# A hybrid decoder block on one core: zero products at the start, a new order of the first loads, and a split last tile

## The chip, the cores and the metric

The kernel runs on one core of a Trainium2 chip. The metric is the device time of one execution in microseconds. Five engines work beside each other, each through its own instructions in order: TensorE (PE: products; PEld: loading of stationary tiles), VectorE (DVE), ScalarE (ACT), GpSimd (POOL) and SyncE (SP, which here only issues transfers). Engines wait for each other and for transfers by semaphores.

## What is computed

One layer of a decoder on 256 tokens with 16 meta tokens ahead of them, width 2048, all in float32:

```
xn = rmsnorm(h, norm1)
u = xn @ w_in                       # 11776 columns: attention q, k, v; retention q, k, v; gates
a = sliding_window_attention(...) @ w_attn_br
r = retention(...) @ w_ret_br
h = h + (sigmoid(gate_a) * a + sigmoid(gate_r) * r) @ w_out
g, up = split(rmsnorm(h, norm2) @ w_gate_up)
h = h + (silu(g) * up) @ w_down
out = rmsnorm(h, norm_f)[:, 128:]   # the meta tokens are dropped
```

## The kernel before

All weights (some 280 MB) are streamed once. Every float32 operand is kept as a high and a low half, and a product of two operands is three products of halves: high by high, high by low, low by high. A `Group` is 512 columns of one weight matrix over its whole contraction. `load` brings chunks of four 128-row contraction tiles by 512 columns (1 MB, three buffers `raw`), `split` makes the halves: ScalarE casts `hi` (L116), VectorE subtracts to get `lo` (L117). `multiply` does half a chunk, a *unit*. For most groups (kind "w") the weights are stationary and 256 or 272 tokens move, and a unit is four contraction tiles by 256 columns; for `w_out` and `w_down` (kind "x") the tokens are stationary and 512 columns move, and a unit is two contraction tiles by 512 columns.

The loop at the end of the kernel goes over all units in order; `ahead` loads and splits some units before they are multiplied. A scheduler then orders each engine's instructions; each engine keeps that order on the chip and waits where a semaphore says so.

The first group (attention keys and values, columns from 1536 of `w_in`) needs the tokens transposed, scaled by `norm1` and split. `norm_chunk(q)` does that for four contraction tiles: per tile one transpose of the 16 meta rows `mt` (L224) and two of the 256 rows of `xt` (L226), into an `aux` buffer (two of these), then ScalarE writes the high half of `xn` (L211) and VectorE the low half (L212). `gains` transposes the norm's weights (L206). The loads of `x` and meta rows come in column ranges between those of the weights, all from SP (L95 to L102, L194 to L200); small tables and the decay table of the retention (`dec`, 1.1 MB, L432) are issued by POOL. `squares` and `norm_end` compute the reciprocal roots `r1`, which the first group's evacuation (`evac_akv`) multiplies in.

At the end, the last group's two token tiles are multiplied one after the other (`toks`), so that the first is finished while the second is multiplied. `evac_down` adds the residual (L630), ScalarE sums squares (L632), `finish` scales and stores (L650 to L662).

## Time and profile before

| | |
|---|---|
| median of 3 runs | 1606.47 us (1604.6 to 1606.73) |
| profiled execution: span from first to last instruction | 1603.7 us |
| profiled execution: own time beside the span | not listed apart |
| PE busy | 1585.0 us, 99% |
| PEld busy | 1390.9 us, 87% |
| DVE busy | 908.6 us, 57% |
| ACT busy | 728.8 us, 45% |
| transfers | 290.64 MB, mean 181 GB/s |

The busy time of PE says that the engine had a product under way, not that it ran at its peak. The span is 2.8 us below the median of the runs. An engine other than PE can matter only where PE waits for it, and such places are found in the list of waits and in the order in time.

### The profile page before, as it was taken

How to read it: one execution, taken by the hardware profiler on the slowest of the kernel's cores; microseconds unless marked ns; L12 is line 12 of the kernel's file. 1: busy time of each engine (PE TensorE's matmuls, PEld its weight loads, DVE VectorE, ACT ScalarE, POOL GpSimd, SP SyncE). 2: the span in 40 equal slices, each digit the busy share in tenths (PEclk: the TensorE clock that was granted, in tenths of full speed). 3: DMA queues.
4: the chain of work that ended last, by engine and by line, in shares of the span. 5: the costliest groups of instructions: out<-in, count | busy, mean ns of one | idle time of the engine just before them, and what ended most of it. 6: DMA issues, size and time to landing. Idle time of an engine off the chain costs nothing.

```text
span 1603.7 us, 22417 instructions
## 1 busy us (share of the span) xinstructions
PE 1585.0 (99%) x9268; PEld 1390.9 (87%) x9268; DVE 908.6 (57%) x1089; ACT 728.8 (45%) x928; POOL 53.4 (3%) x79
## 2 busy tenths in 40 slices
PE   7999999999999999999999999999999999999997
PEld 6999989999988888888888888888888888888886
DVE  4656655465546656565655566656666566454453
ACT  6444444344444444444444444444454444344343
POOL 0212000100000000000000000000000000000000
PEclk9999999999999999999999999999999999999999
DMA  8645444355445555557555555565555656555553
GB/s 276 201 155 168 141 132 132 131 186 182 134 146 194 184 184 185 192 193 245 184 183 175 193 184 185 184 203 190 184 187 185 205 186 210 185 190 194 192 184 105
DMA packets 191702, 290.64 MB, mean 181 GB/s; under 512 B 6289, under 2 KB 98033, under 8 KB 191345
## 3 DMA queue, kind: packets, MB, share of 16 engines
q1 hardware_dynamic: 188480, 280.12, 52.5%
q0 software_dynamic: 1392, 5.94, 1.2%
q10 hardware_dynamic: 1728, 3.16, 0.6%
q8 instruction: 72, 1.18, 0.3%
q14 instruction: 30, 0.24, 0.0%
HBM read 287.08 MB, written 2.12 MB: 180 GB/s over the span
## 4 chain that ended last, share of the span: by engine, by line
PE 96%; DMA 1%; issue 1%; DVE 1%; ACT 0%; SPq 0%; POOL 0%; POOLq 0%; DVEq 0%; ACTq 0%
PE ps L139 34%; PE ps L140 18%; PE ps L159 7%; PE ps L157 7%; PE ps L158 7%; PE ps L145 5%; PE ps L144 5%; PE ps L143 5%; PE ps L137 2%; DMA raw<-in_w_in_dram 1%; PE ps L136 1%; PE aux L407 1%; PE aux L355 1%; PE aux L501 1%; PE aux L385 0%
## 5 line engine op out<-in xcount | busy, mean ns | idle before, releaser
L117 DVE TENSOR_TENSOR lo<-raw,hi 128x1024 fp32r<-128x1024 f32 (+1 forms) x530 | 651.2, 1230 | 541.2 <-ACT hi L116 532.7
L116 ACT CAST hi<-raw 128x1024 fp32r<-128x1024 f32 (+1 forms) x530 | 554.5, 1047 | 683.5 <-PE ps L139 321.8
L139 PE MATMUL ps<-hn,hi 128*128 128x512 f32 x1320 | 460.3, 391 | 0.0
L140 PE MATMUL ps<-hn,lo 128*128 128x256 f32 x1320 | 372.1, 282 | 0.0
L139 PEld LDWEIGHTS ps<-hn,hi 128*128 128x128 f32 x1320 | 247.8, 188 | 51.0
L139 PE MATMUL ps<-xn,hi 128*128 128x512 f32 x720 | 255.1, 396 | 0.0
L140 PEld LDWEIGHTS ps<-hn,lo 128*128 128x128 f32 x1320 | 249.5, 189 | 1.9
L143 PE MATMUL ps<-xn,hi 128*128 128x272 f32 (+1 forms) x704 | 203.1, 291 | 1.5 <-ACT hi L116 1.5
L140 PE MATMUL ps<-xn,lo 128*128 128x256 f32 x720 | 204.2, 284 | 0.0
L144 PE MATMUL ps<-xn,hi 128*128 128x272 f32 (+1 forms) x704 | 203.5, 290 | 0.0
L145 PE MATMUL ps<-xn,lo 128*128 128x272 f32 (+1 forms) x704 | 203.1, 289 | 0.0
L139 PEld LDWEIGHTS ps<-xn,hi 128*128 128x128 f32 x720 | 135.5, 188 | 29.7 <-issue 0.2
L159 PE MATMUL ps<-hi,ff 128*128 128x512 f32 x352 | 139.3, 396 | 0.0
L158 PE MATMUL ps<-lo,ff 128*128 128x512 f32 x352 | 139.3, 396 | 0.0
L157 PE MATMUL ps<-hi,ff 128*128 128x512 f32 x352 | 139.3, 396 | 0.0
L140 PEld LDWEIGHTS ps<-xn,lo 128*128 128x128 f32 x720 | 135.8, 189 | 2.3 <-issue 1.3
L143 PEld LDWEIGHTS ps<-xn,hi 128*128 128x128 f32 x704 | 132.9, 190 | 3.8 <-ACT hi L116 1.9
L144 PEld LDWEIGHTS ps<-xn,hi 128*128 128x128 f32 x704 | 133.5, 190 | 3.0 <-issue 2.8
L145 PEld LDWEIGHTS ps<-xn,lo 128*128 128x128 f32 x704 | 133.4, 190 | 1.9 <-issue 1.8
L541 DVE TENSOR_TENSOR t<-ps,t 128x512 f32<-128x512 f32 x84 | 58.2, 692 | 68.1 <-ACT t L540 68.0
L540 ACT COPY t<-ps 128x512 f32<-128x512 f32 x84 | 49.3, 587 | 86.5 <-PE ps L137 84.0
L139 PE MATMUL ps<-r_hl,hi 128*128 128x512 f32 x240 | 84.1, 394 | 0.0
(198 smaller groups left out, 1496.0 us busy)
## 6 DMA issues: line engine op xcount, KB each, us to landing
raw<-in_w_in_dram SPq DMA_DIRECT2D x91, 1024.0 KB, 5.0
raw<-in_w_gate_up_dram SPq DMA_DIRECT2D x176, 512.0 KB, 4.4
raw<-in_w_down_dram SPq DMA_DIRECT2D x44, 1024.0 KB, 5.0
raw<-in_w_ret_br_dram SPq DMA_DIRECT2D x16, 1024.0 KB, 5.1
raw<-in_w_out_dram SPq DMA_DIRECT2D x16, 1024.0 KB, 5.0
raw<-in_w_attn_br_dram SPq DMA_DIRECT2D x8, 1024.0 KB, 5.0
bias<-tbd POOLq DMA_DIRECT2D x4, 544.0 KB, 8.9
h<-in_x_dram ACTq DMA_DIRECT2D x4, 512.0 KB, 6.1
```

What stands on the lines that cost most here:

```text
L116: g.last_split = nc.scalar.copy(out=hi[:, j], in_=src[:, j])
L117: nc.vector.tensor_tensor(out=lo[:, j], in0=src[:, j], in1=hi[:, j].bitcast(F32), op=ALU.subtract)
L139: mm(out=full, lhsT=wh, rhs=xhl, start=first, stop=False)
L140: mm(out=ps[:, ct, 0:S], lhsT=wl, rhs=xhi, start=False, stop=False)
L143: mm(out=o, lhsT=wh, rhs=xhi, start=first, stop=False)
L144: mm(out=o, lhsT=wh, rhs=xlo, start=False, stop=False)
L145: mm(out=o, lhsT=wl, rhs=xhi, start=False, stop=last)
L157: mm(out=o, lhsT=xlo[:, tok], rhs=hi[:, k, :], start=kt == 0, stop=False)
L158: mm(out=o, lhsT=xhi[:, tok], rhs=lo[:, k, :], start=False, stop=False)
L159: mm(out=o, lhsT=xhi[:, tok], rhs=hi[:, k, :], start=False, stop=kt == nk - 1)
L540: nc.scalar.copy(out=t, in_=ps[:, :, S:2 * S])
L541: nc.vector.tensor_tensor(out=t, in0=ps[:, :, 0:S], in1=t, op=ALU.add)
```

## The change

- *Zero products.* `warm` multiplies a tile of zeros (`idle`, bfloat16, set by VectorE) into a spare accumulator `blank`, nine times ahead of the first transposes and twice behind the first x transposes, in the order of the code.
- *First loads.* In the first group's first chunk the four weight tiles come one by one, with 256 columns of x ahead of the first and the third; later chunks come in halves of two tiles. The meta rows come in two loads from ACT's queue, with 128 partitions each. The decay table is loaded by SP behind the first chunk of group 3, no longer by POOL at the start. `norm2` is loaded later.
- *First units.* For the first group (`pairs`) a unit is two contraction tiles by 512 columns; both accumulators are filled together, and evacuated after the last unit.
- *Meta rows.* Two transposes bring all meta rows (`norm_meta`); one multiply, one cast and one subtraction make their halves for all sixteen contraction tiles. `norm_pair` transposes x alone, two contraction tiles into one `aux` buffer. The meta tokens' norm is summed through a product with a `pick` matrix.
- *Last columns.* The second token tile of the last group is multiplied in two halves of 256 columns (`LAST`), each evacuated by `evac_last`; only the last half stands behind the last product.

In the changed kernel the cast of weights is at L129, the subtraction at L130, the first group's products at L146 to L148, the high half of `xn` at L236 and the low half at L237.

```diff
+    idle = const.tile([128, 512], BF16, name="idle")
+    nc.vector.memset(idle, 0.0)
...
     def load(g, c):
...
+        if g is groups[0]:
+            if c == 0:
+                for k in range(4):
+                    if k % 2 == 0:
+                        load_x(128 * k, 128 * k + 256)
+                    nc.sync.dma_start(out=raw[:, k, :], in_=rows[:, k, c0:c0 + 512])
+            else:
+                load_x(512 * c, 512 * (c + 1))
+                for k in (0, 2):
+                    nc.sync.dma_start(out=raw[:, k:k + 2, :], in_=rows[:, k:k + 2, c0:c0 + 512])
...
+        if g is groups[3] and c == 0:
+            with tc.issue_after(last.ins):
+                nc.sync.dma_start(out=r_state["dec"], in_=c_dec)
...
-    def multiply(g, c, half, toks=(0, 1)):
+    def multiply(g, c, half, toks=(0, 1), a=0, b=512):
...
+        if g.pairs:
+            if c == 0 and half == 0:
+                g.ps = [psm.tile([128, 2, 512], F32, name="ps") for _ in range(2)]
+            for k in range(2):
+                kt = 4 * c + 2 * half + k
...
+                for ct in range(4):
...
+                    mm(out=o, lhsT=wh, rhs=xhi, start=first, stop=False)
+                    mm(out=o, lhsT=wh, rhs=xlo, start=False, stop=False)
+                    m = mm(out=o, lhsT=wl, rhs=xhi, start=False, stop=last)
...
+    blank = psm.tile([128, 2, 512], F32, name="ps")
+    def warm(n):
+        for _ in range(n):
+            mm(out=blank[:, 0, :], lhsT=idle[:, 0:128], rhs=idle, start=True, stop=True)
+    def norm_meta():
+        gains(0, gain1)
+        p = aux()
+        for j in range(2):
+            nc.tensor.transpose(out=p[:, 128 * j:128 * (j + 1)], in_=mq[:, j, :], identity=ident)
+        t = xs.tile([128, KD, NM], F32, name="m_t")
+        nc.vector.tensor_tensor(out=t, in0=p[:, 0:KD * NM].rearrange("p (k m) -> p k m", m=NM),
+                                in1=gain1.unsqueeze(2).broadcast_to([128, KD, NM]), op=ALU.mult)
+        nc.scalar.copy(out=xn[:, :, 0, 0:NM], in_=t)
...
+    def norm_pair(q):
+        p = aux()
+        for k in range(2):
             for t in range(2):
...
+        for k in range(2):
+            kt = 2 * q + k
+            split_t(p[:, 256 * k:256 * (k + 1)], xn[:, kt, :, NM:T], gain1[:, kt:kt + 1])
...
-        nc.gpsimd.dma_start(out=dec, in_=c_dec)
...
+    LAST = ((0, 0, 512), (1, 0, 256), (1, 256, 512))
+    def evac_last(t, a, b, n, ps):
+        h, ss = h_state["h"], const.tile([128, 1], F32, name=f"ss_end{n}")
+        sl = slice(1536 + a, 1536 + b)
+        nc.vector.tensor_tensor(out=h[:, t, sl], in0=ps[:, t, a:b], in1=h[:, t, sl], op=ALU.add)
+        j = ev.tile([128, 512], BF16, name="junk", bufs=1)
+        nc.scalar.activation(out=j[:, 0:b - a], in_=h[:, t, sl], func=AF.Square, accum_out=ss)
+        if b < 512:
+            part = h_state["part"]
+            nc.vector.tensor_tensor(out=part[:, t:t + 1], in0=part[:, t:t + 1], in1=ss, op=ALU.add)
+        else:
+            finish(t, ss)
...
             ahead(4, 0)
-            norm_chunk(0)
-        if i < 8 and half == 0:
+            warm(9)
+            norm_meta()
+            norm_pair(0)
+            warm(2)
+        if i < 8:
             ahead(i + 5, i + 2)
-            if i < 6:
-                norm_chunk(i // 2 + 1)
-            if i > 0:
+            if 0 < i < 7:
+                norm_pair(i + 1)
...
         multiply(g, c, half)
+        if i == 0:
+            with tc.issue_after(g.first_mm.ins):
+                norm_pair(1)
```

The order that the scheduler made of it is shown at three places. A row names the line, the operation, the tiles and their size, and in brackets the semaphores it waits for; DMAHW is a transfer issued by SP or ACT, counted in eight lanes.

TensorE from its first instruction: `g_sb` holds the norm's weights, `mt` and `mq` the meta rows. Before:

```order
L206 MATMUL aux<-ident,g_sb 128x16 [waits DMAHW0_49,Pool_49]
L224 MATMUL aux<-ident,mt 128x16 [waits DMAHW2_49]
L226 MATMUL aux<-ident,xt 128x128 [waits DMAHW1_49]
L226 MATMUL aux<-ident,xt 128x128
L224 MATMUL aux<-ident,mt 128x16 [waits DVE_49]
L226 MATMUL aux<-ident,xt 128x128 x2
L143 MATMUL ps<-xn,hi 128x272 [waits Activation_49]
L144 MATMUL ps<-xn,hi 128x272 [waits DVE_49]
L224 MATMUL aux<-ident,mt 128x16 [waits DMAHW6_49,PE_49]
L226 MATMUL aux<-ident,xt 128x128 [waits DMAHW5_49]
```

And now, behind ten pairs like the first two rows:

```order
L247 LDWEIGHTS idle
L247 MATMUL ps<-idle 128x512
L231 MATMUL aux<-ident,g_sb 128x16 [waits DMAHW0_49,Pool_49]
L254 MATMUL aux<-ident,mq 128x128 [waits DMAHW3_49]
L254 MATMUL aux<-ident,mq 128x128 [waits DMAHW5_49]
L267 MATMUL aux<-ident,xt 128x128 [waits DMAHW1_49,DVE_49]
L267 MATMUL aux<-ident,xt 128x128 x3
L146 MATMUL ps<-xn,hi 128x272 [waits Activation_49]
L146 MATMUL ps<-xn,hi 128x272
L147 MATMUL ps<-xn,hi 128x272 [waits DVE_49]
L148 MATMUL ps<-xn,lo 128x272
```

All eleven zero products stand first; the first x transposes wait for VectorE's copy of the gains, and the second range of x is transposed only behind the first tile's twelve products.

ScalarE from the first activation or cast on: `raw` with 512 columns is one weight tile now, half a unit before. Before:

```order
L211 ACTIVATE xn<-aux,gain_86 128x272 [waits DVE_49,PE_49]
L211 ACTIVATE xn<-aux,gain_86 128x272 [waits PE_49]
L116 CAST hi<-raw 128x512 [waits DMAHW4_49]
L116 CAST hi<-raw 128x512
L211 ACTIVATE xn<-aux,gain_86 128x272 [waits PE_49]
L116 CAST hi<-raw 128x512 [waits DMAHW7_49]
```

And now:

```order
L129 CAST hi<-raw 128x512 [waits DMAHW2_49]
L229 DMA g_sb<-in_norm_dram 16x128
L129 CAST hi<-raw 128x512 [waits DMAHW4_49]
L129 CAST hi<-raw 128x512 [waits DMAHW0_49]
L258 CAST xn<-m_t 128x16x16 [waits DVE_49]
L236 ACTIVATE xn<-aux,gain_88 128x256 [waits PE_49]
L129 CAST hi<-raw 128x512 [waits DMAHW1_49]
L236 ACTIVATE xn<-aux,gain_88 128x256 [waits DVE_49]
```

The casts of the first three weight tiles stand ahead of the meta rows' cast and of the first tile's activations; on VectorE likewise the subtractions of the first two tiles stand ahead of the copy of the gains.

SP's queue from the start. Before:

```order
L199 DMA xt<-in_x_dram 128x2x256
L200 DMA mt<-in_meta_tokens_dram 16x256
L99 DMA raw<-in_w_in_dram 128x4x256
L199 DMA xt<-in_x_dram 128x2x256
L200 DMA mt<-in_meta_tokens_dram 16x256
L102 DMA raw<-in_w_in_dram 128x4x256
L194 DMA xt<-in_x_dram 128x2x512 [waits DMAHW0_49]
L195 DMA mt<-in_meta_tokens_dram 16x512 [waits DMAHW1_49]
L95 DMA raw<-in_w_in_dram 128x4x512 [waits DMAHW2_49]
```

And now:

```order
L225 DMA xt<-in_x_dram 128x2x256
L103 DMA raw<-in_w_in_dram 128x512 x2
L225 DMA xt<-in_x_dram 128x2x256
L103 DMA raw<-in_w_in_dram 128x512 [waits DMAHW0_49]
L103 DMA raw<-in_w_in_dram 128x512 [waits DMAHW1_49]
L225 DMA xt<-in_x_dram 128x2x512 [waits DMAHW2_49]
L107 DMA raw<-in_w_in_dram 128x2x512 [waits DMAHW3_49]
L107 DMA raw<-in_w_in_dram 128x2x512 [waits DMAHW4_49]
```

Two weight tiles stand ahead of the second range of x; the third tile waits for lane 0 (the norm's weights), and the third range of x for lane 2 (the first weight tile).

## Rows read from the trace of the kernel before

**Rows 1.** The page, its first lines: span, and busy time of PE and PEld.
```profile
span 1603.7 us, 22417 instructions
PE 1585.0 (99%) x9268; PEld 1390.9 (87%) x9268; DVE 908.6 (57%) x1089; ACT 728.8 (45%) x928; POOL 53.4 (3%) x79
```

**Rows 2.** Waits of PE, 0 to 20 us: total, times, longest, in us.
```profile
PE aux L224 <- DMA mt<-in_meta_tokens_dram: 3.3, 3, 2.1
```

**Rows 3.** Order in time, PE, 6 to 19 us: start, duration, instruction, idle before.
```profile
7.36 0.60 PE L143 MATMUL ps<-xn,hi 128*128 128x272 f32 x1 [1.54 <-ACT hi L116]
...
12.02 0.43 PE L143 MATMUL ps<-xn,hi 128*128 128x272 f32 x1
12.25 0.43 PE L144 MATMUL ps<-xn,hi 128*128 128x272 f32 x1
...
15.18 0.29 PE L144 MATMUL ps<-xn,hi 128*128 128x272 f32 x1
15.31 0.41 PE L145 MATMUL ps<-xn,lo 128*128 128x272 f32 x2
16.62 0.21 PE L224 MATMUL aux<-ident,mt 16*128 16x16 f32 x1 [0.90 <-DMA mt<-in_meta_tokens_dram]
```

**Rows 4.** Order in time, SP's issues, 0 to 4 us.
```profile
1.74 0.41 SPq L99 DMA_DIRECT2D raw<-in_w_in_dram  x1
2.19 0.51 SPq L199 DMA_DIRECT2D xt<-in_x_dram  x1
...
3.30 0.42 SPq L102 DMA_DIRECT2D raw<-in_w_in_dram  x1
```

**Rows 5.** Transfers issued at 0.74, 1.74, 2.19, 3.30, 3.77 us: KB, us to landing.
```profile
xt<-in_x_dram SPq DMA_DIRECT2D x1, 256.0 KB, 3.1
...
raw<-in_w_in_dram SPq DMA_DIRECT2D x1, 512.0 KB, 4.9
...
xt<-in_x_dram SPq DMA_DIRECT2D x1, 256.0 KB, 7.8
...
raw<-in_w_in_dram SPq DMA_DIRECT2D x1, 512.0 KB, 9.2
...
xt<-in_x_dram SPq DMA_DIRECT2D x1, 512.0 KB, 12.5
```

**Rows 6.** Windows: length, busy of PE, PEld, DVE, ACT, POOL; PEclk, DMA share, GB/s.
```profile
0.00:5.00 5.00, 1.17 (x5) 0.73 (x5) 0.17 (x1) 1.49 (x2) 3.67 (x13) 1.00 0.54 158
5.00:10.00 5.00, 1.64 (x5) 0.88 (x5) 2.29 (x4) 2.11 (x4) 0.00 (x0) 1.00 0.88 235
20.00:25.00 5.00, 5.00 (x39) 4.58 (x39) 3.68 (x5) 4.19 (x11) 0.00 (x0) 1.00 1.05 377
60.00:80.00 20.00, 20.00 (x170) 19.51 (x169) 13.57 (x27) 9.79 (x19) 5.24 (x7) 1.00 0.72 244
```

**Rows 7.** Order in time, ScalarE and VectorE, 5 to 8 us.
```profile
5.02 0.49 ACT L211 ACTIVATE xn<-aux,gain 128x272 fp32r<-128x272 f32 x1 [2.29 <-PE aux L226]
...
6.69 1.14 ACT L116 CAST hi<-raw 128x512 fp32r<-128x512 f32 x2 [0.35 <-DMA raw<-in_w_in_dram]
7.34 1.29 DVE L117 TENSOR_TENSOR lo<-raw,hi 128x512 fp32r<-128x512 f32 x2 [0.46 <-ACT hi L116]
```

**Rows 8.** Chain that ended last, 39 to 41 us: start, length, link.
```profile
39.90 0.16 PE aux L224
40.06 0.37 PE aux L226 x2
```

**Rows 9.** Order in time, 1594 to 1597 us.
```profile
1594.66 0.40 PE L158 MATMUL ps<-lo,ff 128*128 128x512 f32 x1
...
1594.90 0.39 PE L159 MATMUL ps<-hi,ff 128*128 128x512 f32 x1
1595.33 0.69 DVE L630 TENSOR_TENSOR h<-ps,h 128x512 f32<-128x512 f32 x1 [2.06 <-PE ps L159]
1596.05 0.63 ACT L632 ACTIVATE junk<-h 128x512 bf16<-128x512 f32 x1 [2.60 <-DVE h L630]
```

More of the change, by code (lines that the diff above doesn't have):

```diff
@@ L155, in multiply @@
                     tok = slice(t * 128, (t + 1) * 128)
-                    o = g.ps[t][:, t, :]
-                    mm(out=o, lhsT=xlo[:, tok], rhs=hi[:, k, :], start=kt == 0, stop=False)
-                    mm(out=o, lhsT=xhi[:, tok], rhs=lo[:, k, :], start=False, stop=False)
-                    mm(out=o, lhsT=xhi[:, tok], rhs=hi[:, k, :], start=False, stop=kt == nk - 1)
+                    o = g.ps[t][:, t, a:b]
+                    mm(out=o, lhsT=xlo[:, tok], rhs=hi[:, k, a:b], start=kt == 0, stop=False)
+                    mm(out=o, lhsT=xhi[:, tok], rhs=lo[:, k, a:b], start=False, stop=False)
+                    mm(out=o, lhsT=xhi[:, tok], rhs=hi[:, k, a:b], start=False, stop=kt == nk - 1 and b == 512)
     side = deque()
@@ L181, in hybrid_block_kernel @@
     xt = xs.tile([128, 2, D], F32, name="xt")
-    mt = xs.tile([NM, D], F32, name="mt")
     g_sb = xs.tile([16, 2, 128], F32, name="g_sb")
@@ L232, in squares @@
             nc.scalar.activation(out=sq, in_=xt[:, t, sl], func=AF.Square, accum_out=ss1[:, t, q:q + 1])
-        nc.scalar.activation(out=sq[0:NM], in_=mt[:, sl], func=AF.Square, accum_out=ss1[0:NM, 2, q:q + 1])
+        if q == 3:
+            for j in range(2):
+                nc.scalar.activation(out=sq[:, 0:128], in_=mq[:, j, :], func=AF.Square,
+                                     accum_out=ss1[:, 2, j:j + 1])
     def bcast_rstd(pieces, dst):
@@ L252, in norm_end @@
         nc.vector.tensor_reduce(out=ms1[:, 0:2], in_=ss1[:, 0:2, :], axis=mybir.AxisListType.X, op=ALU.add)
-        nc.vector.tensor_reduce(out=ms1[0:NM, 2:3], in_=ss1[0:NM, 2:3, :], axis=mybir.AxisListType.X, op=ALU.add)
         rstd(ms1[:, 0:2], ms1[:, 0:2], D, 2)
-        rstd(ms1[0:NM, 2:3], ms1[0:NM, 2:3], D, 1)
-        bcast_rstd([(ms1[0:NM, 2:3], NM, 0), (ms1[:, 0:1], 128, NM), (ms1[:, 1:2], 128, NM + 128)], r1)
+        nc.vector.tensor_tensor(out=ms1[:, 2:3], in0=ss1[:, 2, 0:1], in1=ss1[:, 2, 1:2], op=ALU.add)
+        pick = xs.tile([128, NM], F32, name="pick")
+        nc.vector.tensor_reduce(out=pick, in_=ident.rearrange("p (q m) -> p m q", m=NM),
+                                axis=mybir.AxisListType.X, op=ALU.add)
+        nc.vector.tensor_scalar(out=pick, in0=pick, scalar1=ms1[:, 2:3], scalar2=None, op0=ALU.mult)
+        p = aux()
+        mm(out=p[:, 0:NM], lhsT=ones, rhs=pick, start=True, stop=True)
+        rstd(r1[:, 0:NM], p[:, 0:NM], D, NM)
+        bcast_rstd([(ms1[:, 0:1], 128, 0), (ms1[:, 1:2], 128, 128)], r1[:, NM:T])
         nc.vector.tensor_scalar(out=r8, in0=r1[:, NM:T], scalar1=0.125, scalar2=None, op0=ALU.mult)
@@ L628, in f @@
             sl = slice(gi * 512, (gi + 1) * 512)
-            for t in ((0, 1) if i is None else (i,)):
+            for t in range(2):
                 nc.vector.tensor_tensor(out=h[:, t, sl], in0=ps[:, t, :], in1=h[:, t, sl], op=ALU.add)
@@ L645, in begin_finish, with finish @@
         nc.vector.tensor_scalar(out=part, in0=part, scalar1=D * EPS, scalar2=None, op0=ALU.add)
-    def finish(t):
-        h, ss, nf = h_state["h"], h_state["ss"], h_state["nf"]
+    def finish(t, last):
+        h, nf = h_state["h"], h_state["nf"]
         ms = const.tile([128, 1], F32, name=f"ms_end{t}")
-        nc.vector.tensor_scalar(out=ms, in0=ss[:, t, 3:4], scalar1=h_state["part"][:, t:t + 1], scalar2=1.0 / D,
+        nc.vector.tensor_scalar(out=ms, in0=last, scalar1=h_state["part"][:, t:t + 1], scalar2=1.0 / D,
                                 op0=ALU.add, op1=ALU.mult)
@@ L752, in ahead @@
             g, c, half = units[loaded]
-            if loaded < 8 and half == 0:
-                load_x(c)
             if half == 0:
@@ L786, in hybrid_block_kernel @@
                 with tc.manual_schedule(engines={mybir.EngineType.PE}):
-                    for t in range(2):
+                    for t, a, b in LAST:
                         for u in units[-4:]:
-                            multiply(*u, toks=(t,))
-                for t in range(2):
-                    g.evac(t, g.ps[t])
+                            multiply(*u, toks=(t,), a=a, b=b)
+                for n, (t, a, b) in enumerate(LAST):
+                    evac_last(t, a, b, n, g.ps[t])
             continue
         multiply(g, c, half)
+        if i == 0:
+            with tc.issue_after(g.first_mm.ins):
+                norm_pair(1)
         if c == g.kt // 4 - 1:
-            if g.kind == "w":
+            if g.pairs and half == 1:
+                for j in range(2):
+                    g.evac(j, g.ps[j])
+            elif g.kind == "w" and not g.pairs:
                 g.evac(half, g.ps[half])
-            elif half == 1:
+            elif g.kind == "x" and half == 1:
                 g.evac(None, g.ps[0])
```

61 lines of the change are left out of this document (28 added, 33 removed).

## The prediction

> **What bounds the kernel now.** I read the page first. TensorE is busy for 1585.0 of 1603.7 us [rows 1], so only the two ends can give time: what TensorE does not do at the start, and what follows its last product. The list of waits then shows TensorE at the start held by loads, one of them for 2.1 us [rows 2]. The order in time shows the rest: a first product at 7.36, then dense products from 12.02, a last stop, and from 16.62 on no gap worth naming [rows 3]; in 20 to 25 us it is busy for 5.00 of 5.00 [rows 6]. Until about 15 us products of 272 columns start every 0.23 us (12.02, 12.25), afterwards every 0.13 (15.18, 15.31) [rows 3]: the two levels of the clock, 1.2 and 2.4 GHz. The granted clock is printed as 1.00 from the start [rows 6], so the spacing has to be read instead. Before the rise the engine had multiplied without a break for some 3 us; the scattered work of 7 to 11 us had raised nothing.
>
> So the question is: from when is TensorE dense, and how much is left to do then? Before: from 16.62, with 21 products of the first group done (the first and last rows are at 7.36 and 15.31 [rows 3]) and four of sixteen contraction tiles transposed. Whatever moves that point moves the end by as much, because nothing later waits.
>
> **When the first product can start.** The products now need the third 128-row tile of weights, though they don't read it: on ScalarE the cast of that tile stands ahead of the two instructions that finish the first activations (second order shown). So I need its landing.
> - The weights' first half (512 KB, issued third) landed at 1.74 + 4.9 = 6.6 us; the second x load at 2.19 + 7.8 = 10.0; the second weight half at 3.30 + 9.2 = 12.5 [rows 4, 5]. In the new SP order the same bytes stand ahead (x 256, two tiles 512, x 256 KB), then the third tile, 256 KB. If nothing gets quicker it lands between 10.0 and 12.5, about 11.2: the upper end.
> - By bytes: through that tile SP moves 1.28 MB, the meta rows 0.13, the small tables some 0.06. The stretch 0 to 5 us moved 158 GB/s x 5 = 0.79 MB, the next 235 GB/s [rows 6]; the remaining 0.68 MB takes 2.9 us: 7.9 us, the lower end. The 1.1 MB decay table and most of the old early traffic behind it no longer compete, but the small constant tables do, and the old x load shows a last piece that comes late.
> - I take 9.0, nearer to the bytes than to the old queue, since the old queue's lateness comes partly from traffic that leaves.
>
> Behind it stand the cast (half of 1.14, so 0.57), the meta cast and the activations of tile 0 (each at most the 0.49 of a 272-wide copy) [rows 7]: 9.0 + 0.57 + 0.49 + 0.49 = 10.5 us. A second gate is earlier: VectorE subtracts two tiles before it copies the gains, on which the transposes wait: 6.6 + 0.57 + 0.65 [rows 7], and some 0.7 for the gains and the meta multiply, is 8.5; two ScalarE copies behind it give 9.5, the floor.
>
> **The sum.**
> - Dense from 10.5 instead of 16.6: -6.1 us.
> - The 21 products are still to do: 21 x 0.13 = +2.7.
> - Transposes: a tile costs 0.16 for the meta rows and 0.37 for x [rows 8]. Left before: 12 x 0.53 = 6.4. Left now: 14 x 0.37 = 5.2, since two meta transposes early replace sixteen. -1.2.
> - The third product waits for VectorE's low half of tile 0, 0.5 after ScalarE's (the nearest row is that copy's 0.49 [rows 7]), of which two products hide 0.2: +0.3.
> - The eleven zero products all stand first on TensorE (first order shown). 512 columns at the slow rate: 0.23 x 512/272 = 0.43 each, 4.7 in all, from about 1.1 to 5.8 us. Before that nothing can be multiplied, since x and weights haven't been split: they cost nothing, and delay three transposes that are not the gate.
> - What they buy is the clock. If it is up at 10.5 us, all rows above hold; if down, the first run is slow as from 12.0 to 14.9 before: 13 products, 0.10 each, 1.3 us. Between them TensorE does only seven transposes in some 4.7 us. No row settles it; I take half, +0.65, and keep 0 and 1.3.
> - Per tile twelve products of 0.13 are 1.6 us; two tiles and their transposes, 3.9. A 1 MB chunk of weights with its 512 KB of x is 4.1 us at 377 GB/s [rows 6] for two such units, so the loads stay ahead once it runs: 0.
> - The decay table goes to SP behind a weight chunk: 1.1 MB, 2.9 us at that rate, in a stretch like 60 to 80 us where DMA is 0.72 busy [rows 6] and weights come two chunks early: 0; without that lead it would cost its 2.9.
> - The end: a product of 512 columns takes 0.23 (1594.66, 1594.90) [rows 9]; two halves take at most 2 x 0.13, so 24 of them cost 0 to 0.7, +0.1 by columns. Behind the last product the add (0.69) and the square (0.63) [rows 9] work on 256 instead of 512 columns. By 272 columns at 0.49 against 512 at 0.63 (ScalarE), and about as much on VectorE, that saves 0.2 to 0.3 each: -0.5. Together -0.4.
> - The pick matrix, one more product of 16 columns and a POOL power on 16 columns replace as many small steps; evacuation has a unit of products ahead of it: 0.
>
> Sum: -6.1 + 2.7 - 1.2 + 0.3 + 0.65 - 0.4 = -4.05 us. The profiled span of 1603.7 would become 1599.6. The median of the three runs is 1606.5, 2.8 above that span; I put the gain on the median: **1602.4 us**.
>
> The Trainium skill gives another price for the third tile ("DMA: Bandwidth & Descriptors", Anatomy of one DMA): about 2.0 us plus the bytes over 436 GB/s, so an estimate of 2.6 us for 256 KB. Issued near 3.5 us it would land at 6.1, the floor of 9.5 would decide, and the sum would be -5.1. The trace speaks against it where several loads are under way: 256 KB took 3.1 us alone and 7.8 behind others [rows 5].
>
> **Rivals.**
> 1. *The third tile comes as late as the old queue.* One piece of the old x load came long after the rest of its bytes could have moved (10.0 against 7.9 by rate). If that repeats, the tile lands at 11.2, products start at 12.75, and the sum loses 2.2: 1604.6. For it: the small tables still run beside it. Against: the decay table and the 1 KB pieces are gone. Chance 0.18.
> 2. *The clock is down when products start, and stays down.* Seven transposes between 6 and 10 us may not keep it up; before, scattered work didn't raise it either. Then 1.65 us are lost in 3.3 us of slow running, or 3.3 in twice that, in place of 0.65: 1603.4 to 1605.0, say 1604.0. Chance 0.18. The Trainium skill states this rule ("TensorE: Matmul & The Clock Gate", What's actually happening): half rate is the default, and idleness brings it back. By that rule the zero products are spent before they are needed, and the time would be this rival's. The trace of before has no such gap inside the run, so it can't confirm it.
> 3. *Slower: the x load behind the weights.* SP holds the next x load (512 KB) until the first weight tile has landed, near 5.3 us, and its transposes stand on TensorE ahead of the third tile's products, reached at about 10.5 + 3.9 = 14.4. The same load took 12.5 us before [rows 5]. If it does so again it lands at 17.8: 3.4 lost, and after such a stop one more slow run, 1.3: 1607.1, slower than before. It decides from a landing after 17.2 (2.8 + 1.3 eat the 4.1); beyond 20.5 the kernel is slower by more than 0.2%. Against: 1.1 MB that ran beside it is gone, and by bytes it lands near 12. Chance 0.06.
>
> **How the numbers follow.** About 0.2%, 3.2 us, is what a measurement of this kernel can tell from no change. The forecast case has 0.58: its own range is 1600.7 (floor of 9.5, clock up) to 1603.1 (clock down for one run). All of that is under 1603.3, so it counts as faster. Rival 1 lies within 0.2%; rival 2 mostly, with 0.02 at its low end faster; rival 3 is 0.04 slower, 0.02 within. Faster 0.60, same 0.36, slower 0.04. The range runs from the forecast case's low end to past rivals 1 and 2, with 0.5 for the scatter of runs: 1600.2 to 1605.5.
>
> **What would show it.** Right: zero products until 5 or 6 us; a first real product between 9.5 and 11.5, held by ScalarE behind the third tile's cast; spacing 0.13 soon after; no TensorE gap over 0.5 us from there; the add after the last product near 0.4 us. Wrong: a first product before 9 (the tile landed early), or after 12.5 (rival 1); products 0.23 apart for over 2 us (rival 2); a wait of TensorE on x after its first products (rival 3). A new stop at the first evacuation, near 45 us, would refute the zero that I gave it.

## The result, and the profile after

The changed kernel takes 1597.5 us (median of 4 runs, 1596.24 to 1598.17) against 1605.84 of the kernel before beside it (4 runs, 1604.6 to 1606.73): ratio 0.9946, interval 0.9934 to 0.9959. That is 8.3 us less, where 4.1 were forecast, and below the range. The profiled execution spans 1595.2 us where before had 1603.7 [rows 1], 8.5 less. The page's first lines:

```profile
span 1595.2 us, 22471 instructions
PE 1580.9 (99%) x9289; PEld 1392.8 (87%) x9289; DVE 910.5 (57%) x1095; ACT 727.8 (46%) x927; POOL 54.2 (3%) x78
```

TensorE is as full as before, yet done 8.5 us earlier. Where it gained is read from the starts of its products, grouped by the tile that they read: engine and operation, count, shortest, median and longest duration in ns, first and last start in us. Of the kernel before:

```profile
L139 PE MATMUL ps<-a_hl,hi x112: 388/392/399, 497.4 to 742.8; 128*128 128x512 f32 x112
L157 PE MATMUL ps<-hi,m x128: 392/394/399, 766.2 to 857.7; 128*128 128x512 f32 x128
L139 PE MATMUL ps<-hn,hi x1320: 389/390/475, 858.4 to 1347.7; 128*128 128x512 f32 x189
L157 PE MATMUL ps<-hi,ff x352: 392/394/399, 1348.7 to 1594.4; 128*128 128x512 f32 x176
L159 PE MATMUL ps<-hi,ff x352: 390/396/399, 1349.2 to 1594.9; 128*128 128x512 f32 x176
```

And of the changed kernel:

```profile
L167 PE MATMUL ps<-a_hl,hi x112: 388/397/398, 493.8 to 740.3; 128*128 128x512 f32 x112
L185 PE MATMUL ps<-hi,m x128: 392/392/395, 763.9 to 853.8; 128*128 128x512 f32 x128
L167 PE MATMUL ps<-hn,hi x1320: 390/390/477, 854.5 to 1343.7; 128*128 128x512 f32 x189
L185 PE MATMUL ps<-hi,ff x360: 279/394/394, 1344.8 to 1586.3; 128*128 128x512 f32 x172, 128*128 128x256 f32 x8
L187 PE MATMUL ps<-hi,ff x360: 279/392/392, 1345.3 to 1586.5; 128*128 128x512 f32 x172, 128*128 128x256 f32 x8
```

First starts subtracted give the time of each stretch, all in us:

| stretch | before | after | gain |
|---|---|---|---|
| to the first a_hl product (the head and the projections) | 497.4 | 493.8 | 3.6 |
| from there to the first m product (the branch outputs) | 268.8 | 270.1 | -1.3 |
| from there to the first hn product (w_out) | 92.2 | 90.6 | 1.6 |
| from there to the first ff product (gate and up) | 490.3 | 490.3 | 0.0 |
| first to last ff product (w_down) | 246.2 | 241.7 | 4.5 |
| last product to the end | 8.8 | 8.7 | 0.1 |

The forecast spoke of the first row (3.65) and the last (0.4). The middle rows were taken as fixed: their instructions, order and tiles are the same in both kernels. Yet w_down's products start closer together, at the same granted clock, as windows over whole stretches show (us, PE busy and count, granted clock, DMA share, GB/s). Before:

```profile
500.00:720.00 220.00, 220.00 (x1258) 1.00 0.56 187
1350.00:1570.00 220.00, 220.00 (x945) 1.00 0.56 191
```

After:

```profile
500.00:720.00 220.00, 220.00 (x1253) 1.00 0.57 190
1350.00:1570.00 220.00, 220.00 (x962) 1.00 0.56 191
```

In w_down 220 us hold 962 products and not 945: 228.7 ns a step and not 232.8. From 500 to 720 us it is the other way, 1253 against 1258, and gate and up do not move (490.3 us in both). DMA moves as much in both, 187 to 191 GB/s.

The head came nearly as described. The zero products run from 1.19 to 6.07 us, ScalarE casts the third tile at 9.60 as soon as it has landed, and the first product follows at 10.95 (10.5 forecast). Then products stand 0.23 apart until 17.28, 0.13 from there (order in time):

```profile
1.19 4.88 PE L247 MATMUL ps<-idle 128*128 128x512 bf16 x11 [1.19 <-DVE idle L74]
7.72 1.09 PE L267 MATMUL aux<-ident,xt 128*128 128x128 f32 x4
9.60 0.62 ACT L129 CAST hi<-raw 128x512 fp32r<-128x512 f32 x1 [2.77 <-DMA raw<-in_w_in_dram]
10.95 0.82 PE L146 MATMUL ps<-xn,hi 128*128 128x272 f32 x2 [2.14 <-ACT xn L236]
12.57 0.43 PE L147 MATMUL ps<-xn,hi 128*128 128x272 f32 x1
12.80 0.43 PE L148 MATMUL ps<-xn,lo 128*128 128x272 f32 x1
17.28 0.30 PE L147 MATMUL ps<-xn,hi 128*128 128x272 f32 x1
```

At the end, where before had one add of 0.69 and one square of 0.63 [rows 9], both halves are now added and squared after the last product:

```profile
1586.55 0.28 PE L187 MATMUL ps<-hi,ff 128*128 128x256 f32 x1
1586.86 0.76 DVE L697 TENSOR_TENSOR h<-ps,h 128x256 f32<-128x256 f32 x2 [2.11 <-PE ps L187]
```

### The profile page after: what moved, and what is told of

It reads as the page before. It is cut to its first block, busy times and chain, and to the rows that moved or that the text cites. A ratio compares the mean times of both kernels' runs of the same rounds, so it can differ in the third digit from the quotient of the medians.

```text
span 1595.2 us, 22471 instructions
## 1 busy us (share of the span) xinstructions
PE 1580.9 (99%) x9289; PEld 1392.8 (87%) x9289; DVE 910.5 (57%) x1095; ACT 727.8 (46%) x927; POOL 54.2 (3%) x78
## 4 chain that ended last, share of the span: by engine, by line
PE 98%; issue 1%; DMA 1%; DVE 0%; ACT 0%; POOL 0%; POOLq 0%; DVEq 0%
PE ps L167 34%; PE ps L168 18%; PE ps L185 7%; PE ps L187 7%; PE ps L186 7%; PE ps L173 5%; PE ps L171 5%; PE ps L172 5%; PE ps L165 2%; PE ps L164 1%; PE aux L461 1%; PE aux L409 1%; PE ps L147 1%; PE ps L146 1%; PE ps L148 1%
## 5 line engine op out<-in xcount | busy, mean ns | idle before, releaser
L130 DVE TENSOR_TENSOR lo<-raw,hi 128x1024 fp32r<-128x1024 f32 (+1 forms) x530 | 651.9, 1230 | 542.3 <-ACT hi L129 533.6
L129 ACT CAST hi<-raw 128x1024 fp32r<-128x1024 f32 (+1 forms) x530 | 555.0, 1047 | 681.5 <-PE ps L167 320.9
L171 PE MATMUL ps<-xn,hi 128*128 128x272 f32 (+1 forms) x640 | 184.9, 289 | 0.0
L173 PE MATMUL ps<-xn,lo 128*128 128x272 f32 (+1 forms) x640 | 184.1, 288 | 0.0
L172 PE MATMUL ps<-xn,hi 128*128 128x272 f32 (+1 forms) x640 | 184.0, 288 | 0.0
L167 PEld LDWEIGHTS ps<-xn,hi 128*128 128x128 f32 x720 | 135.5, 188 | 29.7 <-issue 0.2
L185 PE MATMUL ps<-hi,ff 128*128 128x512 f32 (+1 forms) x360 | 140.0, 389 | 0.0
L187 PE MATMUL ps<-hi,ff 128*128 128x512 f32 (+1 forms) x360 | 139.3, 387 | 0.0
L186 PE MATMUL ps<-lo,ff 128*128 128x512 f32 (+1 forms) x360 | 138.0, 383 | 0.0
L168 PEld LDWEIGHTS ps<-xn,lo 128*128 128x128 f32 x720 | 135.7, 188 | 2.3 <-issue 1.3
L172 PEld LDWEIGHTS ps<-xn,hi 128*128 128x128 f32 x640 | 120.6, 188 | 2.3 <-issue 2.1
L173 PEld LDWEIGHTS ps<-xn,lo 128*128 128x128 f32 x640 | 120.7, 189 | 1.8 <-issue 1.8
L171 PEld LDWEIGHTS ps<-xn,hi 128*128 128x128 f32 x640 | 120.5, 188 | 1.8 <-issue 1.8
```

What stands on the lines that cost most here:

```text
L129: g.last_split = nc.scalar.copy(out=hi[:, j], in_=src[:, j])
L130: nc.vector.tensor_tensor(out=lo[:, j], in0=src[:, j], in1=hi[:, j].bitcast(F32), op=ALU.subtract)
L167: mm(out=full, lhsT=wh, rhs=xhl, start=first, stop=False)
L168: mm(out=ps[:, ct, 0:S], lhsT=wl, rhs=xhi, start=False, stop=False)
L171: mm(out=o, lhsT=wh, rhs=xhi, start=first, stop=False)
L172: mm(out=o, lhsT=wh, rhs=xlo, start=False, stop=False)
```

## The experiments

**Theory A: the place of tiles in SBUF.** The new 1 KB zero tile and some small ones stand ahead of the weights, so everything that grows from the low end (raw, hi, lo, xn, hn, h) lies 1,152 bytes higher; what hangs from the high end (a_hl, r_hl, m, ff) stays. hi moves from byte 44,704 to 45,856, while ff stays at 139,232 and m at 147,424. The groups that changed are those that read one operand from each side. **Rival B:** the step follows the program, by fewer transposes or the third PSUM buffer that turned by one.

### 1. The old kernel, tiles at the new places

```diff
+    pad = const.tile([128, 288], F32, name="pad")
+    nc.vector.memset(pad[:, 0:1], 0.0)
     mhalf = const.tile([128, 8], F32, name="mhalf")
```

> The kernel before with one change: 1,152 bytes per partition that nothing uses, ahead of the tiles of the weights, so that raw, hi, lo, xn, hn and h lie where the changed kernel has them; every instruction and its order stay. Theory A (the place of the moving tiles hi and lo beside the stationary tiles m and ff, which stay where they are, sets the step of the 512-column products): w_down's products start every 228.9 ns as in the changed kernel and not every 233.3, 1056 times 4.4 ns = 4.6 us, w_out 384 times 4.4 = 1.7 us less, the gates about 1 us more; span 1698.0 is not expected, 1598.5 is (1603.7 - 5.2); the stretch 1350 to 1580 us holds about 1006 products where before had 988; the head stays as before, first product at 16.6 us dense. Rival B (the step changed with the order of the program: fewer and other instructions ahead, PSUM buffers turned by one): nothing moves, span 1603.7 within 0.5, 988 products in that stretch.

Measured: 1601.34 us (6 runs), ratio 0.9968 [0.9956, 0.9979]; span 1599.4.

```profile
1350.00:1570.00 220.00, 220.00 (x963) 1.00 0.57 196
```

963 products, where the changed kernel had 962, from an unused pad. By stretches the steps gave 5.0 us, of which this run's head took back 0.6; 4.2 us are left in the medians. That much of the 8.3 us has nothing to do with what the change rewrites. (The clause on 1698.0 in the expectation is a slip of the pen; 1598.5 was the number.)

### 2. The changed kernel, tiles at the old places

```diff
-    idle = const.tile([128, 512], BF16, name="idle")
-    nc.vector.memset(idle, 0.0)
-    mhalf = const.tile([128, NM], F32, name="mhalf")
+    mhalf = const.tile([128, 8], F32, name="mhalf")
...
+    idle = xs.tile([128, 512], BF16, name="idle")
+    nc.vector.memset(idle, 0.0)
+    mhalf16 = xs.tile([128, NM], F32, name="mhalf16")
...
-        h, ss = h_state["h"], const.tile([128, 1], F32, name=f"ss_end{n}")
+        h, ss = h_state["h"], h_state["ends"][:, n:n + 1]
```

> The changed kernel with its new small tiles put elsewhere (the zero tile and the 16-wide exponent in the pool of the head, the ends of the squares in an existing tile), so that raw, hi, lo, xn, hn and h lie again where the kernel before has them; the instructions and the zero products stay. Theory A: w_down and w_out go back to 233 ns a step, 1600.5 us by the profile (1595.2 + 5.3), about 988 products in the 230 us from 1350 us; what is left of the gain, 3.2 us of 8.5, is the head and the end. Rival B: it stays at 1595.2, with 1006 products in that stretch.

Measured: 1602.1 us (9 runs), ratio 0.9978 [0.9968, 0.9987]; span 1601.0.

```profile
1350.00:1570.00 220.00, 220.00 (x944) 1.00 0.56 190
...
11.11 0.62 ACT L127 CAST hi<-raw 128x512 fp32r<-128x512 f32 x1 [4.37 <-DMA raw<-in_w_in_dram]
```

The step is back. This run is the change without its effect on the steps, and so the nearest thing to what was forecast: 1602.1 measured, 1602.4 on record. The forecast counted from 1606.5, though; beside the 1605.55 us of the kernel before in these runs the gain is 3.4 us, and by spans 2.7, where 4.05 were forecast. By spans it lost 5.8 us against the changed kernel: 5.0 through the steps (268.8 + 92.2 + 490.4 + 246.3 against 270.1 + 90.6 + 490.3 + 241.7) and 0.9 in the head, where the third tile could be cast at 11.11 us and not at 9.60, and the first product came at 12.45 and not at 10.95.

### 3. Without the zero products

```diff
-    blank = psm.tile([128, 2, 512], F32, name="ps")
...
-            mm(out=blank[:, 0, :], lhsT=idle[:, 0:128], rhs=idle, start=True, stop=True)
+            pass
...
-            warm(9)
+            warm(0)
             norm_meta()
             norm_pair(0)
-            warm(2)
```

> The changed kernel without its eleven zero products and without the PSUM buffer that they write (no result reads it); the zero tile keeps its place. As predicted, a zero product buys nothing: they end at 5.9 us, the first product waits until 10.95 us for a cast, and the clock rose at 17.3 us, 6.3 us after the first product. Theory A and the prediction's zero price: first product at 10.95, clock up between 16.5 and 18 us, span 1595.2 within 0.5, step still 228.9 ns. Rival C (the zero products shorten the slow stretch): the clock rises later than 18 us and every slow product of 0.227 us instead of 0.125 costs 0.1: up to 5 us more. Rival B (the turned PSUM buffers made the step): the buffers turn as before again, step 233 ns, plus 5 us.

Measured: 1596.81 us (5 runs, 1594.98 to 1596.94), ratio 0.9937 [0.9925, 0.995]; span 1593.1. Not slower: the median is 0.7 us lower, with runs that overlap those of the changed kernel. The profiled execution, the fastest of the five, is 2.1 us faster than the changed kernel's. Its first product came at 9.20 us, not at the expected 10.95, and ScalarE tells why:

```profile
7.67 0.47 ACT L236 ACTIVATE xn<-aux,gain 128x256 fp32r<-128x256 f32 x1 [0.44 <-PE aux L265]
9.20 0.82 PE L146 MATMUL ps<-xn,hi 128*128 128x272 f32 x2 [0.95 <-ACT xn L256]
9.63 0.62 ACT L129 CAST hi<-raw 128x512 fp32r<-128x512 f32 x1 [0.48 <-DMA raw<-in_w_in_dram]
```

The third tile's cast now stands behind the first activations, so the first product no longer waits for that tile. The kernel's scheduler orders ScalarE by its own estimate of times; with zero products ahead of the transposes it put the cast first. PSUM buffers turned as in the kernel before, and w_down kept its 241.7 us (first product at 1342.8, last at 1584.5): rival B is out. The clock was up at 14.7 us, earlier than either theory had it. Experiments 7 and 8 take order and products apart as far as the runs allow.

### 4. The last half in a PSUM bank of its own

```diff
-                    o = g.ps[t][:, t, a:b]
+                    o, new = g.ps[t][:, t, a:b], kt == 0
+                    if a:
+                        o, new = g.ps[2][:, 0, 0:256], (c, half, k) == (units[-4][1], units[-4][2], 0)
...
-                    mm(out=o, lhsT=xhi[:, tok], rhs=hi[:, k, a:b], start=False, stop=kt == nk - 1 and b == 512)
+                    mm(out=o, lhsT=xhi[:, tok], rhs=hi[:, k, a:b], start=False, stop=kt == nk - 1)
...
+            nc.vector.tensor_tensor(out=h[:, t, 1536:2048], in0=ps[:, t, :], in1=h[:, t, 1536:2048], op=ALU.add)
```

> The changed kernel with the end of the second token tile in another form: the last 24 products of its second half go to a PSUM bank of their own, so that the first half's add no longer waits for the very last product; one add of 512 columns and the first half's squares lie beside those 24 products of 0.118 us, and behind the last product only 256 columns are added. If both halves were held to the end by the shared bank (the changed kernel's adds, 0.38 us each, and squares, 0.42 us each, all stand behind the last product): after the last product one add of 0.38 and one square of 0.42 go, and the small add of the parts, some 0.6 to 0.9 us, 1594.4 by the profile. If the end is set by the outgoing transfers alone: no gain, 1595.2.

Measured: 1596.19 us (5 runs, 1595.46 to 1597.57), ratio 0.9938 [0.9924, 0.9952]; span 1594.3. The end in order of time:

```profile
1584.39 0.68 DVE L702 TENSOR_TENSOR h<-ps,h 128x512 f32<-128x512 f32 x1
1585.74 0.42 ACT L704 ACTIVATE junk<-h 128x256 bf16<-128x256 f32 x1 [1.08 <-DVE h L702]
1586.27 0.28 PE L189 MATMUL ps<-hi,ff 128*128 128x256 f32 x1
1586.58 0.42 DVE L700 TENSOR_TENSOR h<-ps,h 128x256 f32<-128x256 f32 x1
```

The first half's add and square run beside the products. From the last product's start to the end it is 8.0 us (1594.3 - 1586.3) and not 8.7. As a gain over the changed kernel it is read from the profile; the runs overlap. In the changed kernel the two halves share a bank, only the very last product carries `stop`, and both adds stand behind it. Whether the first half could be released from a shared bank was not tried.

### 5 and 6. The high side lower by 1,152 and by 512 bytes

```diff
+    low_st, low = open_pool("low", 1, "right")
+    gap = low.tile([128, 288], F32, name="gap")
+    nc.vector.memset(gap[:, 0:1], 0.0)
     a_st, a_pool = open_pool("a", 1, "right")
```

(128 columns for 512 bytes.)

> The changed kernel with 1,152 bytes per partition that nothing uses at the upper end of SBUF, so that a_hl, r_hl, m and ff lie 1,152 bytes lower and stand to hi and lo as in the kernel before, while hi and lo stay where the changed kernel has them. Theory A1 (the distance between the operand on the left side and the one on the right side sets the step): m and ff products go back from 228.9 to 233.3 ns, a_hl and r_hl products from 233.7 and 234.5 to 230.6; xn and hn products (both operands on the left) stay; the stretch 1350 to 1580 us holds 988 products and not 1006; span 1600 (1595.2 + 4.9). Rival A2 (the place of hi and lo by itself): nothing moves, 1006 products, 1595.2.

> The same with 512 bytes. Under A1 the step of the mixed products takes a third value that no run shows yet, between 225 and 236 ns, and xn and hn products stay; under A2 nothing moves (1006 products in 1350 to 1580 us).

Measured: 1601.78 us (7 runs), ratio 0.997 [0.9959, 0.9981], span 1600.6; and 1597.27 us (4 runs), ratio 0.9945 [0.9932, 0.9959], span 1594.7. With 1,152:

```profile
500.00:720.00 220.00, 220.00 (x1259) 1.00 0.57 190
1350.00:1570.00 220.00, 220.00 (x945) 1.00 0.56 191
```

With 512:

```profile
1350.00:1570.00 220.00, 220.00 (x962) 1.00 0.57 191
```

Moving the other operand by the same 1,152 bytes restores the old steps in every group, so it is the distance between the two that counts, not the place of hi and lo. A shift of 512 changes nothing: the third value that was expected of it did not come.

### 7 and 8. Zero products and ScalarE's order apart

```diff
-            g.last_split = nc.scalar.copy(out=hi[:, j], in_=src[:, j])
+            with tc.issue_after(acts[i].ins) if g is groups[0] and (c, half) == (0, 1) else ExitStack():
+                g.last_split = nc.scalar.copy(out=hi[:, j], in_=src[:, j])
```

(7, with zero products: each cast of unit two, the third and fourth tile, behind an activation of xn; `acts` holds these activations.)

```diff
-            warm(9)
-            norm_meta()
-            norm_pair(0)
-            warm(2)
+            warm(0)
+            ahead(5, 2)
+            with tc.issue_after(groups[0].third.ins):
+                norm_meta()
+                norm_pair(0)
```

(8, without: the activations behind the third tile's cast.)

> The changed kernel with its eleven zero products, but ScalarE's casts of the third and fourth weight tile held behind the first and second activation of xn, the order that ScalarE had in the run without zero products. Theory D (what the run without zero products gained was ScalarE's order): the first product stands at 9.2 to 9.6 us and not 10.95, and the gain of about 2.0 us is there with the zero products too: 1593.2 by the profile. Rival E (the zero products themselves cost it, on TensorE): first product at 9.2 to 9.6, but the clock up as late as before, at 17 us, and 1595 by the profile.

> The changed kernel without zero products and with ScalarE's old order (the third tile's cast ahead of the activations). Theory D: first product again behind the third tile, at 10.3 to 11 us, 1595 by the profile. Rival E: 1593. If the zero products help the clock after all, it rises later than 6.3 us after the first product and the span is over 1595.5.

Measured: 7 takes 1595.13 us (5 runs, 1594.47 to 1596.41), ratio 0.9934 [0.9921, 0.9946], span 1592.9; 8 takes 1597.17 (5 runs, 1595.74 to 1597.56), ratio 0.9943 [0.9931, 0.9956], span 1594.6. Beside the changed kernel and experiment 3 that gives four differences:

| | by medians | by profiled spans |
|---|---|---|
| the new order, with zero products | 2.4 less | 2.3 less |
| the new order, without them | 0.4 less | 1.5 less |
| the zero products, in the old order | 0.3 more | 0.6 more |
| the zero products, in the new order | 1.7 less | 0.2 less |

The runs of each of these four kernels lie up to 2 us apart, and only the first of these differences is near to clear of that. With zero products theory D holds: the order alone brought the gain, though the first product came at 10.04 us and not at 9.2 to 9.6, and rival E's clock at 17 us did not come (it was up at 14). Without them the worth of the order is not shown: in 8 the first product came at 11.41, behind the expected 10.3 to 11, and what held it was not the third tile, cast at 9.64, but the meta rows, cast at 10.57 because their second load was late.

But experiment 7 shows that the zero products do something:

```profile
8.55 0.60 PE L270 MATMUL aux<-ident,xt 128*128 128x128 f32 x4
10.04 0.67 PE L147 MATMUL ps<-xn,hi 128*128 128x272 f32 x2 [0.89 <-ACT xn L237]
11.18 0.43 PE L147 MATMUL ps<-xn,hi 128*128 128x272 f32 x1
11.40 0.43 PE L148 MATMUL ps<-xn,hi 128*128 128x272 f32 x1
```

Four transposes take 0.60 us and not the 1.06 to 1.09 of the slow level: the clock was up at 8.5 us. TensorE, which had idled for 1.68 us ahead of the second meta load, then idled for another 0.89 us, and from 10.5 on the products stand 0.23 apart; the granted clock of 10 to 12 us is printed as 0.56. (In the changed kernel's own profiled run the clock had not risen by 7.7 us: four transposes took 1.09.)

### 9 and 10. 64 and 192 bytes

The edit of 5 with 16 and 48 columns.

> The changed kernel with a_hl, r_hl, m and ff 64 bytes lower. So far a shift of 512 left every step alone and one of 1,152 (4 times 256, and 128) put all of them back. Theory A1 in its short form (only the distance within 256 bytes counts, and 128 bytes are the two sides of it): 64 lies between the two, so the m and ff products take a value from 225 to 234 ns; if whole steps of 128 bytes decide, either 228.9 or 233.3, nothing between. xn and hn products stay.

> The same with 192 bytes. If whole steps of 128 bytes decide, it takes the other of the two values than the shift of 64, or the same as one of them; if the distance counts more finely, a further value. A step under 228.4 ns for m and ff, or under 230.5 for a_hl and r_hl, would be a better place than either kernel has.

One run each: 1604.39 us and 1594.01 us beside 1605.37; spans 1602.6 and 1592.2. The times are single ones; the steps are read from the traces, at a granted clock of 1.00. With 64:

```profile
1350.00:1570.00 220.00, 220.00 (x945) 1.00 0.56 190
```

And with 192:

```profile
1350.00:1570.00 220.00, 220.00 (x972) 1.00 0.56 190
```

945 and 972 products: 232.8 and 226.3 ns. 192 bytes give a step that neither kernel had, and with 64 the branch outputs take 269.5 us, between the 268.8 and 270.2 of the shifts by 1,152 and 512: not whole steps of 128 bytes alone count. All the runs by stretch, from first starts as above:

| run | start of hi minus start of ff (or m), within 256 bytes | branch outputs | w_out | gate and up | w_down |
|---|---|---|---|---|---|
| before | 192 | 268.8 | 92.2 | 490.3 | 246.2 |
| after | 64 | 270.1 | 90.6 | 490.3 | 241.7 |
| 1 | 64 | 270.2 | 90.5 | 490.3 | 241.5 |
| 2 | 192 | 268.8 | 92.2 | 490.4 | 246.3 |
| 5 (1,152) | 192 | 268.8 | 92.2 | 490.3 | 246.4 |
| 6 (512) | 64 | 270.2 | 90.5 | 490.3 | 241.8 |
| 9 (64) | 128 | 269.5 | 92.0 | 490.3 | 246.4 |
| 10 (192) | 0 | 270.3 | 89.7 | 490.3 | 239.6 |

For a_hl and r_hl, which lie a multiple of 256 bytes from ff, the same column holds. Equal distances give equal times to 0.3 us, whichever side was moved and in either kernel. In w_out and w_down the distances 128 and 192 differ by no more than 0.2 us. Gate and up, both of whose operands lie on the low side and move together, never change. The distance is taken within 256 bytes because 512 is the only shift tried that changed nothing; 256 by itself was not tried.

### 11. More zero products, up to the first real one

```diff
-            warm(9)
+            warm(14)
...
-            warm(2)
+            with tc.issue_after(groups[0].turned.ins):
+                warm(5)
```

(On top of 7; `turned` is the last transpose of the first x tiles.)

> The changed kernel with ScalarE's casts held behind the activations, and 14 zero products at the start and 5 more behind the last transpose of the first x tiles, so that TensorE is filled up to the first real product. In the run with 11 of them the first product stood at 10.04 us and the clock was up at 14.0, some 16 slow products at 0.227 instead of 0.125: 1.6 us. Theory F (zero products count as little as idle time for the clock): clock up no earlier than 13.5 us, span 1592.9 within 0.7. Rival G (what kept the clock down was the gap between the zero products' end at 5.9 us and the first product): clock up by 11 us, 1591.3.

Measured: 1594.14 us (4 runs), ratio 0.9929 [0.9913, 0.9946]; span 1591.9.

```profile
9.17 1.24 PE L250 MATMUL ps<-idle 128*128 128x512 bf16 x5
10.98 0.29 PE L149 MATMUL ps<-xn,lo 128*128 128x272 f32 x1
11.11 0.29 PE L147 MATMUL ps<-xn,hi 128*128 128x272 f32 x1
```

What rival G expected came: the clock was up by 11 us and the span is nearer to 1591.3 than to 1592.9. With the second set of zero products the clock stays up (1.24 us for five), and the real products stand 0.13 apart from 10.98 on. That gains 1.0 us on experiment 7 by the spans. The medians are 1.0 apart too, but the runs (1593.0 to 1595.97 and 1594.47 to 1596.41) overlap. The edit adds three zero products at the start as well; the two parts were not taken apart.

### 12. What helped, together

Experiments 7, 11 and 4 in one kernel, and the shift by pool:

```diff
     a_hl = a_pool.tile([128, 8, 2, S], F32R, name="a_hl")
+    gap_a = a_pool.tile([128, 40], F32, name="gap_a")
...
+        nc.vector.memset(p.tile([128, 8], F32, name="gap_m")[:, 0:1], 0.0)
...
+        nc.vector.memset(p.tile([128, 48], F32, name="gap_ff")[:, 0:1], 0.0)
```

> What helped, together: the changed kernel with ScalarE's casts held behind the activations and 14 plus 5 zero products (1591.9 by the profile), the last half's products in a bank of their own (0.6 less), m and ff 192 bytes lower (w_out and w_down at about 226.5 ns and not 228.9: 1440 times 2.3 = 3.3 us less), and a_hl and r_hl 160 bytes lower, which is where hn stands to hi within 256 bytes. Theory A1 (the distance alone counts) gives the a_hl and r_hl products hn's step, 229.1 and 118.3 ns, in place of 233.7 and 234.5: 384 times about 5 = 2.0 us less. Sum 1586.0 by the profile, some 2 us more by the clock of the runs, 1588. If the distance is not all, the a_hl and r_hl products lie elsewhere, between 230 and 236, and the profile shows 1588.

Measured: 1590.47 us (4 runs, 1589.8 to 1590.9), ratio 0.9902 [0.9886, 0.9919]; span 1588.6. It beats both kernels: 15 us under before, 7 under the change, which ran at another time.

```profile
L168 PE MATMUL ps<-a_hl,hi x112: 390/390/396, 492.6 to 737.6; 128*128 128x512 f32 x112
L188 PE MATMUL ps<-hi,m x128: 389/389/397, 760.8 to 849.9; 128*128 128x512 f32 x128
9.55 0.48 PE L261 MATMUL aux<-ident,mq 128*128 128x128 f32 x1 [2.42 <-DMA mq<-in_meta_tokens_dram]
10.67 2.27 PE L254 MATMUL ps<-idle 128*128 128x512 bf16 x5
```

The branch outputs take 268.2 us (760.8 - 492.6), the least of all runs. Worked out from the starts of consecutive products of 512 columns, those of r_hl are 229.1 ns apart where hn's are 229.1 too (about 234.5 in the changed kernel, 230.5 before): tiles at the same distance step alike, as theory A1 had it. Of the 2.6 us short of the expected span, 0.5 are steps (4.8 gained on the changed kernel over all stretches, 5.3 expected). The rest is the head: the second meta load came at 9.55 us and not 8.57 as in experiment 11, TensorE idled 2.42 us before it, the clock fell (five zero products took 2.27 us), and the first product came at 12.45 and not 10.23. That load is what the next change should bring forward.

## Why the prediction was wrong

**The direction was right, the size was not. The step that failed** is the first: "TensorE is busy for 1585.0 of 1603.7 us [rows 1], so only the two ends can give time", and with it "nothing later waits". A busy engine can be busy for less long. The sum had no term for the steps in the middle, which took +1.3, -1.6 and -4.5 us: -4.8 together, more than all that the change aimed at. It had no term for the added tiles either, which do no work that TensorE waits for; what they did was to move every tile behind them. Experiments 1, 2 and 5 show it from three sides. Without it (experiment 2) the gain is 3.4 us by the medians and 2.7 by the spans, where 4.05 were forecast.

Term by term:
- **Start of the dense stretch.** 10.95 us for 10.5, third tile ready at 9.6 for 9.0, held by ScalarE as described. That it came so near is in part luck. In the six other profiled runs with the same order of first loads and casts (2, 4, 5, 6, 9 and 10) the third tile's cast starts at 9.40 to 11.44 us and the first product at 10.75 to 12.79, and the head gains 1.6 to 4.1 us. The landing at 6.1 us that the prediction estimates from the Trainium skill ("DMA: Bandwidth & Descriptors", Anatomy of one DMA) came in none of them; the section gives its price for transfers that GpSimd issues, and SP issued this one.
- **"They cost nothing" of the zero products, and "what they buy is the clock", half a price.** Neither half came. What rival 2 describes did, inside the forecast case: the clock was down at the first product and some 20 products ran slow, about 2 us and not 0.65. The rule of the Trainium skill that was weighed there ("TensorE: Matmul & The Clock Gate", What's actually happening: half rate is the default, and idleness brings it back) agrees with experiments 7 and 11: the clock fell where TensorE idled ahead of the first product, and stayed where zero products filled that stretch. That the zero products made the scheduler put a cast first, at about 2 us (experiment 7), was not thought of; the order listing showed the cast there, and the prediction took it as given.
- **The transposes, -1.2: the term that was too small.** That the head gained 3.6 us for the forecast 3.65 is luck: at 20 us both kernels had done 41 real products and transposed six of sixteen tiles, so the changed kernel had gained nothing yet. Its 3.6 us came from 20 to 50 us, and the order in time has nearly all of it. Before:

```profile
20.81 0.29 PE L145 MATMUL ps<-xn,lo 128*128 128x272 f32 x1
21.04 0.23 PE L224 MATMUL aux<-ident,mt 16*128 16x16 f32 x1
21.20 0.44 PE L226 MATMUL aux<-ident,xt 128*128 128x128 f32 x2
...
21.60 0.29 PE L144 MATMUL ps<-xn,hi 128*128 128x272 f32 x1
```

  After:

```profile
20.87 0.29 PE L148 MATMUL ps<-xn,lo 128*128 128x272 f32 x1
21.00 0.60 PE L267 MATMUL aux<-ident,xt 128*128 128x128 f32 x4
21.35 0.50 PE L146 MATMUL ps<-xn,hi 128*128 128x272 f32 x2
21.68 0.29 PE L147 MATMUL ps<-xn,hi 128*128 128x272 f32 x1
```

  Before, two steps between products took 0.79 us with a tile's three transposes among them, and would take 0.25 without: 0.54 a tile, the 0.53 of the prediction. Now three steps take 0.81 and would take 0.375: 0.43 for a *pair* of tiles, where the prediction reckoned 2 x 0.37. Ten tiles before and five pairs now are left at 20 us, 5.4 against 2.2 us: 3.2 of the 3.6. The few products that spread the reciprocal roots (1.0 us before, 0.7 now, worked out in the same way) give 0.3 more.
- **The end, -0.4.** It was -0.1 (8.8 to 8.7). The term let the first half be finished beside the second half's products; in the shared bank both waited for the last product. With a bank of its own for the last half the end gives -0.7 to -0.8 (experiments 4 and 12: 8.0 and 8.1).
- **Zeroes that held:** decay table on SP, evacuation, loads staying ahead. After 20 us TensorE's waits are those of before (0.9, 0.7 and 0.3 us), and gate and up take 490.3 us in both.
- **Rivals 1 and 3** did not come in the profiled execution of the changed kernel. Rival 1's late tile (11.2 us, products from 12.75) nearly or wholly came in experiments 2 and 9: 11.11 and 11.44, products from 12.45 and 12.79. Rival 3 came in no run.

## What to carry to other kernels

When a change allocates anything, note which tiles it moves, and compare the step of unchanged products, by first and last start, before crediting the time to the intended edit; a pad of a few hundred bytes is a cheap control, and a sweep of it a cheap gain. An engine at 99% still has a step that can shrink. Filler products kept the clock here only where they reached to the first real product, and whatever is added ahead can turn a scheduler's order elsewhere. A load that lands 2 us earlier or later from run to run can hide or feign the gain of an edit at the start; a forecast for it needs a range.

## What the runs showed of the hardware

- **TensorE's step depends on where its two operands lie to each other.** Products of 512 columns start every 226.3 to 232.8 ns in w_down, at the granted clock 1.00 and with the same instructions. The effect is not one of more or less DMA: 187 to 196 GB/s in the same stretch. It has opposite signs in the two kinds of group: at the distance where m and ff (the side loaded as weights) are fastest, r_hl and a_hl (the side streamed through) are slow (experiment 10). The Trainium skill names a read port for the weight load that is independent of the streamed operand's ("SBUF — State Buffer", A bandwidth-pool intuition that's wrong (but worth ruling out)). From that alone one would not expect the place to matter; the measurements, 239.6 to 246.4 us for w_down, decide. Why the step follows the distance was not tried and stays open.
- **The granted clock is printed as 1.00 ahead of its first change.** In the changed kernel products stood 0.23 apart from 11 to 17 us under a printed 1.00; where the clock had risen once and fallen, as in experiment 7, the same spacing is printed with 0.56. At the start the spacing tells more than the column.
- **Zero products raise the clock.** Eleven zero products of 0.43 us each, run from 1.2 to 6.1 us, brought it up in six of the eight profiled runs that have them, not in the changed kernel's own and not in experiment 2: transposes took 0.33 us and not 0.47 before any real product had run. In none of the two runs without zero products (3 and 8) did that happen. In all eight the first real products were slow again: TensorE had idled for 0.6 to 3.8 us just ahead of the first one. In experiment 7 that stretch is 0.9 us; in experiment 11 five zero products filled it, and the clock stayed up.
